# An encoder layer on one core: out-projection sums loaded through GpSimd's queue, the convolution paused at the joint of sample and prompt, and three smaller edits

## The chip, the cores and the metric

One core of a Trainium2 chip runs the whole kernel. Its engines are TensorE (PE, matmuls; PEld is its weight loads), VectorE (DVE), ScalarE (ACT), GpSimd (POOL) and SyncE (SP). Each engine works through its own instructions in order and waits on semaphores. SP here only issues DMAs; ACT and POOL issue some too. The metric is the device time of the kernel in microseconds, the median of several runs.

## The reference

One hybrid encoder layer and a final RMS norm, applied to a prompt of 512 tokens and a sample of 1024 tokens with shared weights, all in float32:

```python
h = rms_norm(x, norm_g)
z = h @ w_in
c_val, c_glu, c_gate, q, k, v, a_gate = jnp.split(z, split_points, axis=-1)
...
conv_out = conformer_conv(c_val, c_glu, w_dw, b_dw, ln_g, ln_b, w_pw) * jax.nn.silu(c_gate)
attn_out = banded_sink_attention(q, k, v, sink) * jax.nn.silu(a_gate)
mix = jnp.concatenate([conv_out, attn_out], axis=-1) @ w_out
return x + mix
```

The model width is 2048, `w_in` has 5632 columns, `w_pw` is 1024x1024 and `w_out` 2048x2048. The convolution is depthwise with 31 taps over `c_val * sigmoid(c_glu)`. Attention has 8 heads of 128, 2 key/value heads and a band of 128 tokens. A final RMS norm with its gain `final_norm_g` follows.

## The kernel before

**Numbers.** Every float32 operand is split into a high and a low part (`parts`, L506: ACT writes the high part, DVE subtracts to get the low one), and each product is three matmul passes: high by high, high by low, low by high. A weight pair of both parts is called `hl`, a token pair `t`.

**Units and jobs.** For the sample and its out-projection, a `Unit` computes a 2x2 block product by seven products instead of eight, P1 to P7, each of 12 matmuls of 128x512. It holds three PSUM banks; P6, P7 and P4 add onto P1's bank, so a bank must be read (`tap`) before the next product onto it. The prompt uses a `Job`: one output block, 48 matmuls over 16 input blocks, with the weights split in two halves (`preps`, L397). The run (L640) is: the sample's input projection in four stages of units (stages 0 to 3), the prompt's jobs `pj` for its input projection, the sample's pointwise jobs, the out-projection units `over[0]` and `over[1]` (eight each, one pass over each half of the inner dimension), the prompt's pointwise jobs, and `last_run` (L1776), the prompt's out-projection with its final norm.

**Sums of two passes.** A unit's result must be added to something. In the input projection the second pass adds the first pass's stored partial with an accumulating DMA on POOL's queue (`add_into`, L500); what follows (scale by the token's norm, sigmoid or silu, store) is put on the list `later` and run by `turn_over` (L542) after `landing` turns (4), one turn per product. At the start of each job the list is flushed entirely. In the out-projection, `Onto` (L270) instead loads the addend first: pass 0 loads the residual x (`xT_s`), pass 1 the stored partial (`part_out`). `begin` (L282) allocates a 128x512 tile, alternately from the pools G and U of four buffers each (`E`, L477), and issues the load on SP. `product` calls it `ahead` products before the one that needs it (2; 0 for the first two units of `over[1]`, which run interleaved). `tap` (L301) then adds the bank onto that tile (L304), and the result is stored on SP.

**Order on the queues.** SP carries nearly every load and store, in an order set when the program is built. Among them are the stores of sums of `w_out` blocks (`wsum_P`, made by DVE at L143 and reused by `last_run`), the token sums (`msum_S`, `mix_d`; L878) and the weights (`raw`).

**Work beside the matmuls.** Three lanes (`Lane`) hold the convolution, the attention and preparations. At each tick a lane gets credit in proportion to its `rate` and emits steps while it has any; `pace` sets a rate at the start of a unit or job. The sample's convolution runs as DVE steps at L1032 and L1040 (128x512 each). Its rate is 0.3 in stage 3 and RATES[3] = 1.0 from the prompt's first job on. `until` forces it to its end at the start of job `pj[18]`.

**The joint.** The sample's last unit is called `end`. During its first four products the prompt's 16 token blocks are split (`follow`, L514 and L515). Its first prompt job has `behind` set: the splits of its weights are ordered behind the last ACT and DVE instructions of the turn before (`marks`). At the start of that job the attention of the sample is put on its lane; its query blocks are loaded by `load_query` (L1145) into U tiles and split on ACT at L510.

**The start.** The constant `norm_g` is loaded first on SP, then the weights and tokens of the first unit; 20 small matmuls (`warm`) run on PE meanwhile.

**The end.** In `last_run` the last product P4 closes rows 2 and 3 of four row blocks, one after the other; rows 0 and 1 wait in `pending`. `complete` (L1730) squares the last quarter, finishes the norm factor `s` with one Newton step, and scales and stores the row in two halves of 128x1024 (L1754 to L1759).

Of the kernel before, what the change touches and what calls it, by code (L numbers as in the profile page):

```python
# [7 lines left out]
F32 = mybir.dt.float32  # L8
F32R = mybir.dt.float32r
AF = mybir.ActivationFunctionType  # L10
ALU = mybir.AluOpType
# [259 lines left out]
class Onto(Unit):  # L271
# [10 lines left out]
    def begin(self, n):  # L282
        if n not in self.d:
            self.d[n] = self.e.E()
            self.e.nc.sync.dma_start(self.d[n], self.source(*n))

    def open(self):
        super().open()
# [97 lines left out]
class Job:  # L386
# [10 lines left out]
    def preps(self, e):  # L397
        def one(k):
            st = {}
            i = slice(k, k + 2 * HALF)  # L400

            def load():
                st["raw"] = e.A([2, HALF, P], F32) if self.early and k else e.raw_tile()
                e.nc.sync.dma_start(st["raw"], self.w[:, i, :])
                if self.low and k:

                    low, c = self.low
                    t = st["hl"] = e.hl_tile()
                    if c == 0:
                        e.nc.sync.dma_start(t[:, 1].bitcast(F32).rearrange("p a b c -> p (a b) c"), low[:, i, :])  # L410
                    else:
                        e.nc.sync.dma_start(t[:, 1, 1].bitcast(F32), low[:, k + HALF : k + 2 * HALF, :])

            def make():
                raw = st.pop("raw")
                if "hl" in st:
                    t = st.pop("hl")
                    e.nc.scalar.activation(t[:, 0], raw, AF.Copy)
                    if self.low[1]:
                        e.nc.vector.tensor_tensor(t[:, 1, 0], raw[:, 0], t[:, 0, 0].bitcast(F32), ALU.subtract)  # L420
                    return t
                t = e.hl_tile()
                e.parts(t[:, 0], t[:, 1], raw)
                return t

            return Prep(load, make, behind=self.behind)

        return [one(self.ks[q]) for q in range(0, len(self.ks), 2 * HALF)]


class Encoder:
# [129 lines left out]
    def constants(self):  # L561
# [4 lines left out]
            nc.sync.dma_start(t, a[key])  # L566
            return t

        self.norm_g = load("norm_g", [ND])
        self.ones = self.const.tile([P, P], F32, name="ones")  # L570
        nc.vector.memset(self.ones, 1.0)
        self.ones_r = self.const.tile([P, P], F32R, name="ones_r")
# [984 lines left out]
class LastPost(Post):  # L1557
# [136 lines left out]
    def load_rows(self):  # L1694
# [4 lines left out]
        self.gain = {}  # L1699
        self.sq = [e.small(4) for _ in range(NB)]  # L1700
        self.rest = [e.small(1) for _ in range(NB)]
        self.load_columns(0, e.A)

    def load_columns(self, c, room):
# [23 lines left out]
    def complete(self, b, c, odd):  # L1728
# [4 lines left out]
        self.seen[b] = n + 1  # L1733
        junk = e.G().rearrange("p (i x) -> p i x", x=P)
        nc.scalar.activation(junk, y, AF.Square, accum_out=self.sq[b][:, n : n + 1])
        if n < 3:
            nc.vector.tensor_tensor(y, y, self.gain[c, odd], ALU.mult)
        sq, rest = self.sq[b], self.rest[b]
        if n == 2:
            nc.vector.tensor_tensor(rest, sq[:, 0:1], sq[:, 1:2], ALU.add)  # L1740
            nc.vector.tensor_tensor(rest, rest, sq[:, 2:3], ALU.add)
            nc.vector.tensor_scalar(rest, rest, 1.0 / D, RMS_EPS, ALU.mult, ALU.add)
        if n == 3:
            s, v, t = e.small(1), e.small(1), e.small(1)
            nc.scalar.activation(s, sq[:, n : n + 1], AF.Sqrt, scale=1.0 / D, bias=rest)
            nc.vector.tensor_scalar(v, sq[:, n : n + 1], 1.0 / D, rest, ALU.mult, ALU.add)
            nc.vector.reciprocal(s, s)
            nc.vector.scalar_tensor_tensor(t, s, s, v, ALU.mult, ALU.mult)
            nc.vector.tensor_scalar(t, t, -0.5, 1.5, ALU.mult, ALU.add)
            nc.vector.tensor_tensor(s, s, t, ALU.mult)  # L1750
            half = self.half
            for h in range(2):
                other, last = (self.blocks(self.rows[b], h, o) for o in (1 - odd, odd))
                nc.scalar.activation(other, other, AF.Identity, scale=s)  # L1754
                if h == c:
                    nc.vector.scalar_tensor_tensor(last, last, s, self.gain[c, odd], ALU.mult, ALU.mult)
                else:
                    nc.vector.tensor_scalar(last, last, s, None, ALU.mult)
                nc.sync.dma_start(self.out[b * P : (b + 1) * P, h * half : (h + 1) * half], self.rows[b][h])  # L1759

    ADDS = {
        "P1": ((0, 0),), "P2": ((0, 0),), "P6": ((0, 1),), "P5": ((1, 1),),
# [12 lines left out]
    def last_run(self, at):  # L1775
# [5 lines left out]
        for c in range(2):  # L1781
            bank = [None] * 3
            for name in ENDS[c]:
# [25 lines left out]
                if end:  # L1809
# [48 lines left out]
def encoder(ctx, tc, a):  # L1858
# [27 lines left out]
    def first():  # L1886
# [273 lines left out]
```

## Time and profile before

| | us |
|---|---|
| median of 3 runs | 2083.21 (2081.64 to 2086.21) |
| profiled execution, its own time | 2080.18 |
| span of its instructions | 2078.4 |
| PE busy | 2060.7 |
| DVE busy | 1754.4 |
| ACT busy | 1043.6 |
| POOL busy | 122.6 |
| mean granted TensorE clock | 0.997 |

The profile is of one execution. A row of a timeline gives start, length, engine, source line, operation, the tiles written and read, and in brackets how long the engine was idle before it and what ended that. Rows of `SPq`, `ACTq` and POOL's `DMA_DIRECT2D` are issues of DMAs, not transfers. The length of a matmul reaches past the start of the next one, so differences of starts are used for rates.

### The profile page before, as it was taken

Reading aid. Unit: us, or ns where it says so; the run is one execution under the profiler, and the core shown is the slowest. Engines: PE = TensorE matmul, PEld = TensorE weight load, DVE = VectorE, ACT = ScalarE, POOL = GpSimd, SP = SyncE. Lnnn points to the kernel's source line nnn. Section 1 sums busy time; section 2 is a strip of 40 time slices with the busy share of each in tenths; the row PEclk is TensorE's granted clock in tenths of the full one; section 3 lists DMA queues with packets and bytes.
Section 4 is the critical chain, followed back from the end, with each engine's and each line's share of the span. In section 5 each row is a group of like instructions: output and inputs, shape, how many; then the busy total and the mean of one; then the engine's idle time right before and its main releaser. Section 6 shows DMA issues by size and latency. Waiting matters only on the chain.

```text
span 2078.4 us, 27092 instructions
## 1 busy us (share of the span) xinstructions
PE 2060.7 (99%) x9259; PEld 1699.2 (82%) x9259; DVE 1754.4 (84%) x2873; ACT 1043.6 (50%) x1711; POOL 122.6 (6%) x176
## 2 busy tenths in 40 slices
PE   9999999999999999999999999999999999999998
PEld 8888888888888888788888888888888887888886
DVE  8767899998899999999666877767799977998887
ACT  7485445333464434554455777336454343454454
POOL 0111111111111111100000000000000000000000
PEclk9999999999999999999999999999999999999999
DMA  8888886864577767954455555996789899678897
GB/s 288 312 298 256 199 223 221 285 220 160 188 242 192 175 169 183 280 166 156 153 172 187 177 182 183 315 330 234 247 289 300 278 299 293 220 247 298 289 333 277
DMA packets 245819, 494.55 MB, mean 238 GB/s; under 512 B 23600, under 2 KB 84400, under 8 KB 245680
## 3 DMA queue, kind: packets, MB, share of 16 engines
q1 hardware_dynamic: 225136, 445.62, 63.9%
q0 software_dynamic: 19392, 45.10, 9.4%
q10 hardware_dynamic: 1152, 2.10, 0.3%
q8 instruction: 72, 1.18, 0.2%
q14 instruction: 67, 0.55, 0.1%
HBM read 331.77 MB, written 160.96 MB: 237 GB/s over the span
## 4 chain that ended last, share of the span: by engine, by line
PE 48%; DVE 7%; issue 6%; DMA 4%; ACT 2%; POOL 1%; SPq 0%; ACTq 0%; POOLq 0%; DVEq 0%
PE a L669 13%; PE a L207 7%; PE c L669 6%; PE b L669 6%; PE c L207 3%; PE pv L1196 2%; PE a L1835 2%; PE s L1167 2%; PE s L1835 2%; PE b L207 1%; PE pt L1201 1%; DVE hl L511 1%; DVE f L1003 1%; DVE t L511 1%; DVE f L1040 1%
## 5 line engine op out<-in xcount | busy, mean ns | idle before, releaser
L207 PE MATMUL a<-t,hl 128*128 128x512 f32 x2640 | 633.6, 391 | 4.7 <-DVE u L304 3.2
L207 PEld LDWEIGHTS a<-t,hl 128*128 128x128 f32 x2640 | 494.7, 188 | 110.6 <-DVE u L304 3.6
L510 ACT ACTIVATE hl<-raw 128x1024 fp32r<-128x1024 f32 (+3 forms) x334 | 296.1, 890 | 384.5 <-PE c L207 81.6
L511 DVE TENSOR_TENSOR hl<-raw,hl 128x1024 fp32r<-128x1024 f32 (+3 forms) x334 | 338.8, 1015 | 145.8 <-ACT hl L510 144.4
L669 PE MATMUL a<-t,hl 128*128 128x512 f32 x1344 | 328.0, 394 | 0.0
L207 PE MATMUL c<-t,hl 128*128 128x512 f32 x1320 | 319.2, 389 | 0.0
L207 PEld LDWEIGHTS c<-t,hl 128*128 128x128 f32 x1320 | 247.3, 188 | 51.6 <-DVE u L304 0.4
L669 PEld LDWEIGHTS a<-t,hl 128*128 128x128 f32 x1344 | 248.6, 188 | 49.8
L1040 DVE SCALAR_TENSOR_TENSOR f<-f,c_w_dw,f 128x512 f32<-128x512 f32 x248 | 173.9, 750 | 0.3
L669 PE MATMUL b<-t,hl 128*128 128x512 f32 x672 | 164.6, 395 | 2.2 <-DVE hl L511 2.2
L1003 DVE SCALAR_TENSOR_TENSOR f<-f,c_w_dw,f 128x512 f32<-128x512 f32 x232 | 163.7, 748 | 1.2 <-ACT f L998 1.2
L669 PE MATMUL c<-t,hl 128*128 128x512 f32 x672 | 164.2, 393 | 0.3 <-DVE hl L511 0.3
L207 PE MATMUL b<-t,hl 128*128 128x512 f32 x660 | 160.0, 389 | 0.0
L669 PEld LDWEIGHTS b<-t,hl 128*128 128x128 f32 x672 | 126.1, 190 | 28.0 <-DVE hl L511 2.6
L669 PEld LDWEIGHTS c<-t,hl 128*128 128x128 f32 x672 | 124.7, 188 | 25.5 <-DVE hl L511 0.7
L207 PEld LDWEIGHTS b<-t,hl 128*128 128x128 f32 x660 | 123.7, 188 | 25.6
L1032 DVE SCALAR_TENSOR_TENSOR f<-f,w_both,f 128x512 f32<-128x512 f32 x120 | 90.0, 750 | 2.1
L236 ACT ACTIVATE u<-a 128x512 f32<-128x512 f32 x82 | 48.7, 594 | 66.8 <-PE a L207 64.2
L236 ACT ACTIVATE g<-a 128x512 f32<-128x512 f32 x78 | 46.3, 594 | 69.1 <-PE a L207 64.6
L1181 ACT ACTIVATE p<-p,tiny 128x384 f32<-128x384 f32 (+1 forms) x96 | 54.5, 570 | 39.8 <-DVE tiny L1178 27.3
L510 ACT ACTIVATE a<-pt 128x512 fp32r<-128x512 f32 x64 | 37.9, 593 | 66.3 <-PE pt L1201 66.2
L511 DVE TENSOR_TENSOR a<-pt,a 128x512 fp32r<-128x512 f32 x64 | 44.1, 689 | 27.3 <-ACT a L510 26.6
(350 smaller groups left out, 2687.9 us busy)
## 6 DMA issues: line engine op xcount, KB each, us to landing
raw<-w_in SPq DMA_DIRECT2D x170, 512.0 KB, 5.3
raw<-w_out SPq DMA_DIRECT2D x31, 512.0 KB, 5.0
raw<-w_pw SPq DMA_DIRECT2D x24, 512.0 KB, 4.2
wsum_P<-raw SPq DMA_DIRECT2D x47, 256.0 KB, 3.3
raw<-wsum_P SPq DMA_DIRECT2D x18, 512.0 KB, 5.0
f<-x_s SPq DMA_DIRECT2D x16, 512.0 KB, 8.2
g<-wsum_P SPq DMA_DIRECT2D x28, 256.0 KB, 4.2
a<-sum_S SPq DMA_DIRECT2D x24, 256.0 KB, 6.2
```

What stands on the lines that cost most here:

```text
L207: nc.tensor.matmul(acc, hl[:, l, o, j, :], toks[j][:, r], start=name in FRESH and j == 0 and q == 0, stop=name in LAST and j == HALF - 1 a ...
L236: nc.scalar.activation(t, bank, AF.Copy)
L510: nc.scalar.activation(hi, x, AF.Copy)
L511: nc.vector.tensor_tensor(lo, x, hi.bitcast(F32), ALU.subtract)
L669: nc.tensor.matmul(job.acc[0], hl[:, l, kk // HALF, kk % HALF, :], r, start=i == 0 and p == 0, stop=i == nk - 1 and p == 2,)
L1003: nc.vector.scalar_tensor_tensor(t, h[:, j : j + T], w(j), t, ALU.mult, ALU.add)
L1032: nc.vector.scalar_tensor_tensor(m0, odd[:, j : j + H], both(j), m0, ALU.mult, ALU.add)
L1040: nc.vector.scalar_tensor_tensor(out, d[:, j : j + H], w(2 * j + k), out if j else m0, ALU.mult, ALU.add)
L1167: nc.tensor.matmul(ps[:, 0:n], qs[:, x, h], k[y][:, keys], start=p == 0, stop=p == 2)
L1181: nc.scalar.activation(p[:, 0:n], p[:, 0:n], AF.Exp, bias=nm[:, h : h + 1], accum_out=l[:, h : h + 1])
L1196: nc.tensor.matmul(pv, v[x][:, vs], pt[:, y], start=i == 0 and p == 0, stop=i == last and p == 2)
L1835: nc.tensor.matmul(acc[t], self.toks[name, m][:, x, i, t * P : (t + 1) * P], parts[i][l].rearrange("p a b -> p (a b)"), start=fresh and fi ...
```

## The change

Seven edits in one diff:

1. `Onto.begin` issues its load on POOL's queue instead of SP's, and the first two units of `over[1]` begin their loads one product ahead instead of none.
2. The convolution's rate is 0 from the start of `end`, and RATES[3] is set at the third prompt job instead of the first.
3. The first half of the first prompt job's weights is no longer ordered behind the marks; the second half still is.
4. `landing` of `end` is 8 instead of 4. The result of its P2, the only one that four turns brought to an end within `end`, is now finished in the flush at the first job's start.
5. `norm_g` is loaded on ACT's queue instead of SP's.
6. 17 warm-up matmuls instead of 20.
7. In `last_run`, the norm factor takes one DVE step less on its chain (the factor -0.5 is folded in ahead, in `less`); scaling is a function of its own, `scale`, which splits the finished half of a row between DVE and ACT and stores it as two quarters, then the other half. Its calls for row 1 and later rows are ordered behind the add and the square of the row that just finished.

```diff
@@ Onto.begin
-            self.e.nc.sync.dma_start(self.d[n], self.source(*n))
+            self.e.nc.gpsimd.dma_start(self.d[n], self.source(*n))
@@ Job.preps
-            return Prep(load, make, behind=self.behind)
+            return Prep(load, make, behind=self.behind and k > 0)
@@ Encoder.constants
-        self.norm_g = load("norm_g", [ND])
+        self.norm_g = self.const.tile([P, ND], F32, name="c_norm_g")
+        nc.scalar.dma_start(self.norm_g, a["norm_g"])
@@ LastPost.complete
+            nc.vector.tensor_scalar(self.less[b], rest, -0.5, None, ALU.mult)
         if n == 3:
             s, v, t = e.small(1), e.small(1), e.small(1)
             nc.scalar.activation(s, sq[:, n : n + 1], AF.Sqrt, scale=1.0 / D, bias=rest)
-            nc.vector.tensor_scalar(v, sq[:, n : n + 1], 1.0 / D, rest, ALU.mult, ALU.add)
+            nc.vector.tensor_scalar(v, sq[:, n : n + 1], -0.5 / D, self.less[b], ALU.mult, ALU.add)
             nc.vector.reciprocal(s, s)
             nc.vector.scalar_tensor_tensor(t, s, s, v, ALU.mult, ALU.mult)
-            nc.vector.tensor_scalar(t, t, -0.5, 1.5, ALU.mult, ALU.add)
-            nc.vector.tensor_tensor(s, s, t, ALU.mult)
...
+            nc.vector.scalar_tensor_tensor(s, t, 1.5, s, ALU.add, ALU.mult)
+            return lambda: self.scale(b, c, odd, s)
+
+    def scale(self, b, c, odd, s):
+        nc, half = self.e.nc, self.half
+        out = self.out[b * P : (b + 1) * P]
+        x, at = self.rows[b][1 - c], (1 - c) * half
+        nc.vector.tensor_scalar(x[:, : half // 2], x[:, : half // 2], s, None, ALU.mult)
+        nc.scalar.activation(x[:, half // 2 :], x[:, half // 2 :], AF.Identity, scale=s)
+        for h in range(2):
+            cols = slice(h * (half // 2), (h + 1) * (half // 2))
+            nc.sync.dma_start(out[:, at + cols.start : at + cols.stop], x[:, cols])
+        other, last = (self.blocks(self.rows[b], c, o) for o in (1 - odd, odd))
+        nc.vector.scalar_tensor_tensor(last, last, s, self.gain[c, odd], ALU.mult, ALU.mult)
+        nc.scalar.activation(other, other, AF.Identity, scale=s)
+        nc.sync.dma_start(out[:, c * half : (c + 1) * half], self.rows[b][c])
@@ LastPost.last_run
-                    for args in pending:
-                        e.urgently(self.complete, *args)
+                    scales = [e.urgently(self.complete, *args) for args in pending]
                     pending.clear()
+                    e.urgently(scales.pop(0))
...
                         finished(t)
-                        e.urgently(self.complete, *pending.pop())
+                        added = nc.cur_bb.bb.instructions[-1]
+                        scales.append(e.urgently(self.complete, *pending.pop()))
+                        squared = self.squared
+                        while scales:
+                            with e.tc.issue_after(added), e.tc.issue_after(squared):
+                                e.urgently(scales.pop(0))
@@ encoder
-        e.warm(20, True)
+        e.warm(17, True)
...
-    end.look = NHL - 1
+    end.look, end.landing = NHL - 1, 8
...
-    pace(pj[0], RATES[3])
+    pace(end, 0.0)
+    pace(pj[2], RATES[3])
...
     for u in over[1][:2]:
-        u.ahead = 0
+        u.ahead = 1
```

More of the change, by code (lines that the diff above doesn't have):

```diff
@@ L1701, in load_rows @@
         self.rest = [e.small(1) for _ in range(NB)]
+        self.less = [e.small(1) for _ in range(NB)]
         self.load_columns(0, e.A)
@@ L1735, in complete @@
         nc.scalar.activation(junk, y, AF.Square, accum_out=self.sq[b][:, n : n + 1])
+        self.squared = nc.cur_bb.bb.instructions[-1]
         if n < 3:
@@ L1745, in complete @@
             nc.scalar.activation(s, sq[:, n : n + 1], AF.Sqrt, scale=1.0 / D, bias=rest)
-            nc.vector.tensor_scalar(v, sq[:, n : n + 1], 1.0 / D, rest, ALU.mult, ALU.add)
+            nc.vector.tensor_scalar(v, sq[:, n : n + 1], -0.5 / D, self.less[b], ALU.mult, ALU.add)
             nc.vector.reciprocal(s, s)
             nc.vector.scalar_tensor_tensor(t, s, s, v, ALU.mult, ALU.mult)
-            nc.vector.tensor_scalar(t, t, -0.5, 1.5, ALU.mult, ALU.add)
[L1750 to L1759, printed above, removed]
+            nc.vector.scalar_tensor_tensor(s, t, 1.5, s, ALU.add, ALU.mult)
[13 more added lines that the diff above has]
+        nc.sync.dma_start(out[:, c * half : (c + 1) * half], self.rows[b][c])
     ADDS = {
```

## The prediction

> **What bounds the kernel now.** I read the page first, then the granted clock by stretches, then TensorE's timeline with the releaser of each wait in brackets, and last the other engines' timelines around those waits and at both ends.
>
> ```profile
> span 2078.4 us, 27092 instructions
> PE 2060.7 (99%) x9259; PEld 1699.2 (82%) x9259; DVE 1754.4 (84%) x2873; ACT 1043.6 (50%) x1711; POOL 122.6 (6%) x176
> ```
>
> TensorE (PE) sets the time: it is busy for all but 17.7 us of the span, start and tail included. A change that removes no matmul can only win what PE loses in waits, in slow clock and at the two ends. The clock by stretches (columns: busy time of PE, weight loads, DVE, ACT, POOL; clock; DMA share; GB/s):
>
> ```profile
> 860.50:864.00 3.50, 3.50 (x10) 2.70 (x9) 3.50 (x6) 1.31 (x2) 0.88 (x1) 0.51 1.05 268
> ...
> 1729.60:1734.30 4.70, 4.63 (x13) 3.66 (x14) 4.37 (x9) 0.74 (x2) 0.00 (x0) 0.64 0.74 238
> ```
>
> The granted clock drops to half in these two places, and PE's timeline shows a wait just before each:
>
> ```profile
> 842.95 3.02 PE L207 MATMUL a<-t,hl 128*128 128x512 f32 x12 [1.07 <-ACT g L236]
> ...
> 1716.53 2.88 PE L207 MATMUL b<-t,hl 128*128 128x512 f32 x12
> 1719.25 2.88 PE L207 MATMUL s<-t,hl 128*128 128x512 f32 x12
> ...
> 859.49 12.36 PE L669 MATMUL b<-t,hl 128*128 128x512 f32 x46 [2.19 <-DVE hl L511]
> 871.69 6.29 PE L669 MATMUL a<-t,hl 128*128 128x512 f32 x27
> ...
> 1729.67 4.43 PE L207 MATMUL a<-t,hl 128*128 128x512 f32 x12 [3.23 <-DVE u L304]
> 1733.89 2.44 PE L207 MATMUL s<-t,hl 128*128 128x512 f32 x9
> ```
>
> A product of 12 matmuls takes 1719.25-1716.53 = 2.72 us, 0.227 a matmul. After the wait of 3.23 us the next 12 take 1733.89-1729.67 = 4.22, so 1.50 more is lost: **4.7 us** at this place, in the out-projection. After the 2.19 us wait 46 matmuls take 12.20 where 46 x 0.227 = 10.44 would do: 1.76 more, **3.95** in all, at the prompt's first job. The wait of 1.07 at 842 is not followed by such a stretch.
>
> The Trainium skill (TensorE: Matmul & The Clock Gate, section "Why this matters for your kernels") warns of idle gaps above about 3 us. By it the gap of 2.19 would cost no clock, and my sum would be 1.8 smaller; the row at 860.50 reads 0.51, so the trace decides against that bound here.
>
> **Part 1: sums loaded on POOL's queue (`Onto.begin`), and one step earlier in two units.** What was late at 1726 was a load, and its queue shows why:
>
> ```profile
> 1718.81 1.57 SPq L504 DMA_DIRECT2D wsum_P<-raw  x2
> ...
> 1721.22 0.39 SPq L504 DMA_DIRECT2D wsum_P<-a  x1
> 1721.67 1.75 SPq L878 DMA_DIRECT2D p<-mix_d  x2
> 1723.46 0.43 SPq L285 DMA_DIRECT2D u<-part_out  x1
> ...
> 1725.37 0.69 DVE L511 TENSOR_TENSOR t<-p,t 128x512 fp32r<-128x512 f32 x1
> 1728.92 0.69 DVE L304 TENSOR_TENSOR u<-a,u 128x512 f32<-128x512 f32 x1 [2.85 <-DMA u<-part_out]
> ```
>
> `u<-part_out` stands on SP behind stores of `wsum_P`, each of which waits for a DVE subtraction (L143). The sum it reads was stored a whole pass earlier, so I put the delay down to the queue. POOL has no other work in this stage. All 64 loads (16 units of 4) move, each freeing SP of an issue like the 0.43 above, which wins nothing by itself. On POOL such a load has no row, so I bound it:
>
> ```profile
> L268 POOL DMA_DIRECT2D part_q<-u x16 | 8.6, 540 | 68.4 <-DVE u L257 61.8 <-ACT u L236 6.6
> L501 POOL DMA_DIRECT2D u<-part_q x16 | 15.0, 940 | 63.0 <-DVE u L257 55.2 <-issue 7.8
> ...
> DMA to landing us min/median/max: 3.8/5.5/9.0
> ...
> u<-part_out SPq DMA_DIRECT2D x16, 256.0 KB, 4.4
> ...
> part_out<-u SPq DMA_DIRECT2D x16, 256.0 KB, 3.1
> ```
>
> An issue costs POOL between 0.54 (a plain store, L268) and 0.94 (an accumulating load, L501), 35 to 60 us in all, on an idle engine. The landing lies between SP's median of 4.4 for the same load and the slowest 9.0 of POOL's accumulating ones (third row, of L501); a plain load is nearest to SP's, and I take 5. The lead: a load is begun two products ahead (5.44), the product itself takes 2.72, and its bank is written again a product later (2.72), less the add's 0.69: 10.2 us. Even 9.0 is covered. In the two interleaved units `ahead` goes from 0 to 1, one step of two products, 5.44 more; the price is a G or U buffer held that much longer, on POOL's own queue.
>
> With the load in time, DVE does L304 at 1726.06 instead of 1728.92; PE has stood since 1729.67-3.23 = 1726.44 and goes on near 1726.7. Of 4.7, 0.3 stays: I take **4.4**. Next DVE could be late: without idle time it is 2.86 ahead of before, while PE is 4.7 ahead, so up to 1.9 could come back. Bounds 2.8 to 4.7.
>
> **Part 2: the joint between sample and prompt.** Four edits meet here: the convolution paused, the first weights freed of their place behind marks (`behind and k > 0`), `landing` 8 for the last sample unit, RATES[3] set at the third job.
>
> ```profile
> 838.89 0.63 ACT L510 ACTIVATE hl<-p 128x512 fp32r<-128x512 f32 x1 [1.15 <-DVE p L143]
> ...
> 842.32 0.57 ACT L236 ACTIVATE g<-a 128x512 f32<-128x512 f32 x1
> ...
> 855.74 0.69 DVE L974 TENSOR_TENSOR g<-g,f 128x512 f32<-128x512 f32 x1 [1.00 <-DMA g<-part_gate]
> 858.21 1.22 DVE L511 TENSOR_TENSOR hl<-raw,hl 128x1024 fp32r<-128x1024 f32 x1
> ...
> L1040 DVE SCALAR_TENSOR_TENSOR f<-f,c_w_dw,f 128x512 f32<-128x512 f32 x10 | 7.2, 750 | 0.0
> ...
> L1032 DVE SCALAR_TENSOR_TENSOR f<-f,w_both,f 128x512 f32<-128x512 f32 x2 | 1.5, 744 | 0.0
> ```
>
> The wait of 1.07 is for ACT's L236, queued behind a weight split that waited 1.15 for DVE, which had convolution steps in front. Without them that wait goes: worth about 1.07, at least 0. The wait of 2.19 is for DVE's L511, the low part of the first weights. DVE idled 1.00 before it for an accumulating DMA: L974 was emitted ahead. With `landing` 8 that sum is finished only in the flush at the job's start, behind L511, and the weights may go earlier: 2.19 and the clock's 1.76 go. Upper bound 1.07+3.95 = 5.0.
>
> Something else is late next. PE would enter the second job at 871.69-5.0 = 866.7. Its weights are ready at:
>
> ```profile
> 865.39 0.63 ACT L510 ACTIVATE a<-u 128x512 fp32r<-128x512 f32 x1 [3.58 <-DMA u<-q_d]
> 865.93 0.71 ACT L514 ACTIVATE t<-a,c_norm_g 128x512 fp32r<-128x512 f32 x1
> ...
> 869.21 1.22 DVE L511 TENSOR_TENSOR hl<-raw,hl 128x1024 fp32r<-128x1024 f32 x1
> ```
>
> ACT stands 3.58 us on the query load `u<-q_d`, and behind it are the prompt's last tokens (L514) and the second job's weights, low part ready at 870.4. The third matmul of that job wants them at 867.1: up to 3.3 late, less 0.6 for a convolution step that leaves DVE's row. I expect two shorter waits (tokens, then weights) of 2.2 together and no halved clock: 5.0-2.2 = **2.8**, bounds 0.3 to 5.0.
>
> The paused work is not gone: the ten L1040 and two L1032 above, 7.2+1.5 = 8.7 us of DVE between 838 and 882, run later. Cover:
>
> ```profile
> 1000.00:1053.00 53.00, 53.00 (x252) 44.10 (x251) 23.72 (x50) 25.38 (x47) 0.00 (x0) 1.00 0.46 149
> ```
>
> DVE is idle for 29 us there, and the forced finish comes only at the prompt's nineteenth job. Without the cover those 8.7 us would stand once in front of a job.
>
> **Part 3: the start.**
>
> ```profile
> 0.74 0.39 SPq L566 DMA_DIRECT2D c_norm_g<-norm_g  x1
> 1.19 0.42 SPq L325 DMA_DIRECT2D raw<-w_in  x1
> ...
> 3.21 0.31 ACT L510 ACTIVATE hl<-raw 128x128 fp32r<-128x128 f32 x1 [1.19 <-DMA raw<-w_in]
> ```
>
> With `norm_g` on ACT's queue every SP issue comes 0.45 earlier. ACT pays one issue, about SP's 0.39, inside its 1.19 of idle time. Three warm-up matmuls fewer make room for it. I take **0.4**, bounds 0 (landing set by bandwidth) to 0.45.
>
> **Part 4: the tail.**
>
> ```profile
> 2072.58 0.16 DVE L1750 TENSOR_TENSOR tiny<-tiny,tiny 128x1 f32<-128x1 f32 x1
> 2072.78 0.72 ACT L1754 ACTIVATE a<-a,tiny 128x512 f32<-128x512 f32 x1 [0.86 <-DVE tiny L1750]
> ...
> 2072.78 0.49 DVE L1758 TENSOR_SCALAR a<-a,tiny 128x512 f32<-128x512 f32 x1
> ```
>
> One tiny step of the chain goes: 2072.78-2072.58 = 0.20, less some 0.06 because the one that stays is a longer form. ACT's two passes stay, so the last store leaves 0.14 earlier; the first bytes leave after DVE's 0.49 instead of ACT's 0.72, with the 0.14 some 0.37 earlier. I take **0.25** between the two. Four more stores cost SP issues, which nothing waits for. The added `less` steps, four of about 0.2, come a product or more before the end, under its matmuls; uncovered they cost 0.8.
>
> **Sum.** 4.4+2.8+0.4+0.25 = 7.85. The profiled execution took 2080.18 (span 2078.4), so it would be 2072.3; the median shown, 2083.21, is 3.0 higher, so **2075.4**. Own range, from the bounds: gains 3.2 (2.8+0.3+0+0.1) to 10.5 (4.7+5.0+0.45+0.37), 2072.7 to 2080.0.
>
> **Rivals.**
>
> A, the wait moves to the second job: the query load holds 2.7 us in one piece and the clock halves again, 1.76. Part 2 gains 0.5, the rest 5.05: 2077.7. For it: ACT's 3.58. Against: tokens come first and split the wait.
>
> B, the load is earlier but the add is not: L304 is placed where it was, behind other DVE work of a saturated engine. Part 1 gains nothing: 2083.21-3.45 = 2079.8. Against: DVE really idled 2.85 for it. With A as well (C): 1.15 left, 2082.1.
>
> D, slower: POOL's loads come late. One mechanism: in POOL's in-order queue a load waits for its buffer's store to land (the 3.1 of `part_out<-u`), then takes the slowest 9.0: 12.1, which is 1.9 beyond the lead of 10.2. Once in each of the second pass's eight units: 15.2 lost, 3.45 won elsewhere, 2095.0. It decides from the second late unit on. For it: 9.0 was seen. Against: the sums are begun in every unit two products ahead.
>
> The Trainium skill (SBUF — State Buffer, "SBUF: two separate sides") says a DMA from GpSimd's queue can wait for descriptors while DVE runs certain copies; that would feed D. In this trace POOL's issues last 0.54 to 0.94 beside a busy DVE.
>
> **How the numbers follow.** Forecast 0.48, A 0.22, B 0.10, C 0.07, D 0.13. About 0.2% (4.2 us) is what a measurement of this kernel can tell from no change. Faster means below 2079.0: forecast and A, 0.70. B and C lie within 4.2 of 2083.21: same, 0.17. Slower is D, 0.13, and it alone is left out of the range, which takes in A, B and C and 2 us below the forecast's own for runs as far apart as those of before (2081.64 to 2086.21): 2070.5 to 2082.5.
>
> **What would show it.** Right: no TensorE wait on L304 near 1720, a clock of 1.00 there, POOL issues through the out-projection, no L1040 between the last unit's start and the third job. Wrong: a wait on `hl` L511 or `t` L515 with the halved clock in the second job (A), a DVE wait on `part_out` issued by POOL (D), L304 still late with its load landed (B).

## The result, and the profile after

The changed kernel takes 2078.75 us (median of 13 runs, 2074.16 to 2084.51) against 2082.3 for the kernel before in the same comparison (13 runs, 2080.57 to 2087.39). The ratio is **0.9979, 95% interval 0.9971 to 0.9987**: 4.4 us faster, 2.7 to 6.0. In a second comparison (`e4_after` below) it is 0.9966 (0.9953 to 0.9978).

The profiled execution of the changed kernel is its fastest, 2074.16 with a span of 2072.4, so the two profiles differ by 6.0 us where the medians differ by less. From its page:

```profile
span 2072.4 us, 27195 instructions
PE 2057.6 (99%) x9256; PEld 1696.0 (82%) x9256; DVE 1752.3 (85%) x2873; ACT 1043.9 (50%) x1711; POOL 157.8 (8%) x240
```

TensorE is 3.1 us less busy with three small matmuls fewer (half clock counts as busy), and POOL has 64 instructions more, the loads. The joint, in TensorE's timeline of the changed kernel:

```profile
843.07 3.01 PE L207 MATMUL a<-t,hl 128*128 128x512 f32 x12 [1.07 <-ACT g L236]
...
858.10 10.50 PE L670 MATMUL b<-t,hl 128*128 128x512 f32 x44 [0.53 <-DVE hl L511]
869.41 0.73 PE L670 MATMUL b<-t,hl 128*128 128x512 f32 x2 [0.81 <-DVE t L515]
```

The wait of 1.07 near 842 has not moved. The wait of 2.19 is 0.53 (the 44 matmuls start 0.227 apart), and a wait of 0.81 for the last token's low part is new. The out-projection, same view, and then the clock over both places (columns as before):

```profile
1705.42 5.72 PE L207 MATMUL a<-t,hl 128*128 128x512 f32 x24 [0.24 <-DVE u L304]
...
1723.30 2.58 PE L207 MATMUL s<-t,hl 128*128 128x512 f32 x10 [0.41 <-DVE hl L511]
```

```profile
857.00:864.00 7.00, 6.47 (x28) 5.05 (x29) 3.60 (x5) 3.01 (x5) 0.88 (x1) 1.00 1.10 310
1722.00:1736.00 14.00, 13.59 (x60) 10.81 (x59) 13.12 (x21) 3.80 (x6) 1.65 (x3) 1.00 0.99 318
```

The wait of 3.23 us is gone, waits of 0.24 and 0.41 are what is left between 1700 and 1745, and the clock is 1.00 at both places. POOL's loads, the group of `begin`'s line in the changed kernel (ns min/median/max, first and last start), and their landing:

```profile
L285 POOL DMA_DIRECT2D u<-part_out x16: 546/546/548, 1683.8 to 1834.4; - x16
...
DMA to landing us min/median/max: 2.7/4.9/6.8
```

On SP the first load of `part_out` started at 1723.46 (in the prediction); on POOL it starts 40 us earlier, at 1683.8.

### The profile page after: what moved, and what is told of

Same layout as the page of the kernel before. It is cut to its first block, busy times and chain, and to the rows that moved or that the text cites. A ratio compares the mean times of both kernels' runs of the same rounds, so it can differ in the third digit from the quotient of the medians.

```text
span 2072.4 us, 27195 instructions
## 1 busy us (share of the span) xinstructions
PE 2057.6 (99%) x9256; PEld 1696.0 (82%) x9256; DVE 1752.3 (85%) x2873; ACT 1043.9 (50%) x1711; POOL 157.8 (8%) x240
## 3 DMA queue, kind: packets, MB, share of 16 engines
q0 software_dynamic: 24512, 61.88, 12.1%
## 4 chain that ended last, share of the span: by engine, by line
PE 52%; issue 7%; DVE 4%; DMA 2%; POOL 1%; ACT 1%; POOLq 0%; ACTq 0%; SPq 0%; DVEq 0%
PE a L670 14%; PE c L670 7%; PE b L670 7%; PE a L207 7%; PE c L207 3%; PE s L1168 2%; PE pv L1197 2%; PE s L1851 2%; PE a L1851 2%; PE b L207 1%; PE pt L1202 1%; DVE hl L511 1%; PE pt L1851 1%; PE pv L1851 1%; POOL u L501 1%
## 5 line engine op out<-in xcount | busy, mean ns | idle before, releaser
L236 ACT ACTIVATE u<-a 128x512 f32<-128x512 f32 x82 | 48.7, 594 | 69.7 <-PE a L207 66.9
L236 ACT ACTIVATE g<-a 128x512 f32<-128x512 f32 x78 | 46.4, 595 | 70.0 <-PE a L207 65.1
L418 ACT ACTIVATE hl<-raw 128x1024 fp32r<-128x1024 f32 x43 | 45.4, 1056 | 47.1 <-PE a L670 18.7
```

The lines of the kernel that those rows point to most:

```text
L236: nc.scalar.activation(t, bank, AF.Copy)
```

## The experiments

All kernels are compared with the kernel before by the same two matmuls of the program, counted among the 128x512 ones. The table gives how much longer (+) or shorter a stretch took than in the first profile of the kernel before; 838 to 905 is the joint, 1700 to 1745 the turn from the first to the second pass of the out-projection. The tail is the time from the last matmul's start to the end of the span. Each ratio is against the kernel before in the same comparison; the stretches are read from one profile each.

| kernel | first product at | joint | out-projection | tail | ratio to before, interval |
|---|---|---|---|---|---|
| before | 5.65 | 0 | 0 | 9.02 | |
| e5_before, again | 5.65 | -0.42 | -0.43 | 8.71 | |
| e1_sums | 5.64 | -2.46 | -4.83 | 9.87 | 0.9968 (0.9956 to 0.9981) |
| e10_queue | 5.65 | +0.51 | -3.73 | 8.74 | 0.9980 (0.9971 to 0.9989) |
| e2_joint | 5.64 | -2.66 | -0.95 | 9.15 | 0.9985 (0.9975 to 0.9994) |
| e3_ends | 5.00 | -1.99 | -0.17 | 9.37 | 0.9989 (0.9981 to 0.9998) |
| changed kernel | 5.01 | -2.82 | -3.46 | 9.21 | 0.9979 (0.9971 to 0.9987) |
| e4_after, again | 5.01 | -2.94 | -3.91 | 9.56 | 0.9966 (0.9953 to 0.9978) |
| e9_no_landing | 5.01 | -1.25 | -3.04 | 9.28 | 0.9974 (0.9964 to 0.9984) |
| e14_no_pause | 5.01 | +1.69 | -3.03 | 9.02 | 0.9989 (0.9979 to 0.9998) |
| e6_pause_early | 5.01 | -4.08 | -2.72 | 9.34 | 0.9968 (0.9956 to 0.9981) |
| e7_no_flush | 5.01 | -4.01 | -2.72 | 9.29 | 0.9958 (0.9944 to 0.9971) |
| e13_both | 5.01 | -4.62 | -1.93 | 9.29 | 0.9957 (0.9943 to 0.9971) |

### The kernel before, once more

> The kernel before, unchanged, for a second profile. In the runs of one part alone the stretch from 40 to 838 us was 1.9 to 3.3 us longer than in the first profile of the kernel before, and the joint, which those runs of edit 1 and of edits 5 to 7 do not touch, lost 2.0 to 2.5 us less: the wait near 859 was 1.95 to 1.99 us there and no half clock followed, where it followed the wait of 2.19. Theory: the kernel before itself varies in the same way, so this profile has waits on L236 near 84, 103 or 163 that the first did not have, and a joint that halves the clock only if its wait is 2.1 us or more. Rival: the first profile is what the kernel before always does, and the longer waits came from the edits.

The kernel before varies from execution to execution, as the theory had it. From 40 to 838 us this execution took 3.6 us longer than the first profile; of that 0.44 and 0.46 were lost at small waits on L236 near 84 and 103. Its joint waited 1.68 us and kept the full clock (by the same brackets e1_sums and e3_ends waited 1.78 and 1.82; the expectation counts from the starts of matmuls). In the out-projection TensorE waited longer than in the first profile:

```profile
1734.86 3.02 PE L207 MATMUL a<-t,hl 128*128 128x512 f32 x12 [3.35 <-DVE u L304]
```

and no half clock followed, against the prediction's reading that such a wait brings one. The windows of this execution around the wait, cut every 3.413 us from the place where its clock halved in the tail, show how the wait lies:

```profile
1729.80:1733.21 3.41, 1.71 (x8) 1.09 (x6) 1.76 (x3) 1.08 (x2) 0.00 (x0) 1.00 0.85 247
1733.21:1736.63 3.42, 1.77 (x8) 1.47 (x9) 2.52 (x5) 1.34 (x3) 0.00 (x0) 1.00 0.83 298
```

The same cut in the first profile of the kernel before, where the half stretches started at 860.55 and 1730.95, 870.40 us or 255 times 3.413 apart:

```profile
857.14:860.55 3.41, 1.22 (x6) 0.89 (x6) 3.41 (x5) 2.38 (x4) 0.86 (x1) 1.00 1.06 330
860.55:863.96 3.41, 3.41 (x10) 2.64 (x9) 3.41 (x6) 1.26 (x2) 0.88 (x1) 0.50 1.04 266
1727.54:1730.95 3.41, 1.28 (x6) 1.06 (x7) 2.03 (x4) 1.15 (x2) 0.00 (x0) 1.00 0.70 251
1730.95:1734.36 3.41, 3.41 (x10) 2.64 (x9) 3.08 (x6) 0.80 (x2) 0.00 (x0) 0.50 0.92 295
```

Six matmuls in a window and the next is at half clock; eight in each of two windows and nothing happens, though the wait was longer. The next kernel measures this by itself.

### Forty holds: what halves the clock

```diff
+    def hold(self):
...
+        nc.tensor.matmul(spin, self.ones_r, self.ones_r, start=True, stop=True)
+        with self.tc.high_priority(URGENT):
+            nc.scalar.activation(z, spin[:, :32], AF.Copy)
+            for _ in range(5 + n % 8):
+                nc.scalar.activation(z, z, AF.Copy)
+        nc.tensor.matmul(spin[:, :32], self.ones_r, z, start=True, stop=True)
```

> The kernel before with 40 holds added to prompt jobs 3 to 42: in the middle of each job TensorE waits for a chain of 6 to 13 small ACT copies before the next product, so that idle times of some 1 to 4 us stand at many phases. It measures the halved clock by itself. In ten profiles so far every half-clock stretch began a whole number of 3.413 us after another, and the stretch ahead of each had 2.0 us or more of idle time inside it (2.0, 2.1, 2.3, 2.5, 3.0), while a wait of 3.5 us that lay across two stretches with 1.87 and 1.78 us halved nothing. Theory: time runs in stretches of 3.413 us on a fixed grid, and a stretch with over 2.0 us of TensorE idle time is followed by one at half clock; all half stretches of this run lie on one grid and idle time per stretch separates halving from not at 2.0 +- 0.1 us. Rival (the length of one gap decides): every single gap above 2.2 us is followed by half clock wherever it lies. Rival (about 3 us decides): only gaps above 3 us are.

The 40 holds and the waits of the kernel itself made 26 stretches at half clock, the tail's among them, every one a whole number of 3.413 us from the tail's start. Three windows of this kernel on that grid, each with the next; the first two are followed by half clock, the third is not:

```profile
987.07:990.48 3.41, 1.39 (x7) 0.94 (x5) 3.40 (x8) 1.89 (x6) 0.00 (x0) 1.00 0.67 229
990.48:993.89 3.41, 0.00 (x0) 0.00 (x0) 3.06 (x7) 3.19 (x15) 0.00 (x0) 0.50 0.15 56
1239.65:1243.07 3.42, 1.60 (x9) 1.16 (x8) 0.00 (x0) 2.13 (x9) 0.00 (x0) 1.00 0.85 261
1243.07:1246.48 3.41, 3.41 (x10) 2.63 (x9) 0.00 (x0) 0.00 (x0) 0.00 (x0) 0.50 0.00 0
1522.96:1526.37 3.41, 1.56 (x8) 1.11 (x6) 0.28 (x1) 1.93 (x8) 0.00 (x0) 1.00 1.00 320
1526.37:1529.79 3.42, 2.83 (x13) 2.35 (x14) 0.00 (x0) 0.47 (x3) 0.00 (x0) 1.00 0.98 303
```

By TensorE's idle time in these rows the theory's border of 2.0 +- 0.1 us fails: the second window was idle for 1.82 us (3.42 less 1.60) and halved the next, the third for 1.85 and did not. Counted by the matmuls' width the border is sharp. At half clock a 128x512 matmul starts every 0.427 us, so at full clock its 512 columns are taken as half of that, 0.213. Over the windows of 14 profiles (from 12 us on, the tail left out) that ran at full clock themselves, the 32 that were followed by half clock hold at most 1.25 us of columns, and the 8412 that were not hold at least 1.24: the border is at about 1.25 us, just under six wide matmuls, where fifteen start in a window without waits (3.413 by 0.227). So it is neither the length of a gap (3.35 us halved nothing, 2.19 did) nor 3 us, but how a gap lies on the grid, and two gaps in one window add up. Both single-gap rivals fall. That it is columns that count and not busy time is seen again in `e13_both`.

### Edit 1 alone, and its queue alone

```diff
-            self.e.nc.sync.dma_start(self.d[n], self.source(*n))
+            self.e.nc.gpsimd.dma_start(self.d[n], self.source(*n))
...
-        u.ahead = 0
+        u.ahead = 1
```

> The kernel before with edit 1 alone: the addends of the out-projection are loaded on POOL's queue, and the first two units of the second pass begin theirs one product ahead. Theory (the load's place in SP's queue is the whole cause): no TensorE wait on L304 above 0.5 us between 1700 and 1740, granted clock 1.00 there, 3.2 to 3.5 us gained at that place and nothing elsewhere, so a profiled execution near 2076.9; the joint keeps its waits of 1.07 and 2.19 us and its half clock. Rival (the gain there needs the other edits, which change when the interleaved units start): the wait of about 3 us on L304 or on L511 comes back, and less than 1.5 us is gained. Rival (POOL's loads are sometimes late): a wait on a load of part_out issued by POOL in the second pass, time no better than before.

> The kernel before with POOL's queue for the addends of the out-projection alone; the first two units of the second pass still begin their loads with the product that needs them (ahead 0). In five profiles with both halves of edit 1 no add L304 waits for a DMA by more than 0.1 us; in the four with the loads on SP each has 3 to 7 such waits. Theory (the queue is the cause, ahead adds a margin that is not needed): no add waits more than 0.3 us for part_out near 1730, the joint of the two passes (1700 to 1745) 2.5 to 4.5 us shorter than in the kernel before. Rival (ahead is the cause): L304 still waits 1 us or more for part_out near 1730, gain there below 1.5 us.

The out-projection is 4.83 shorter with both halves and 3.73 with the queue alone. No wait on L304 above 0.39 us is left there and the clock is 1.00, so the queue is the cause, as the theory of both runs says, and `ahead` is not needed: with the queue alone the first load of `part_out` starts at 1691.5, also some 30 us before SP's. The rest of what was expected of `e1_sums` missed: more was gained there than 3.2 to 3.5, the joint waited 1.78 us instead of 2.19 and kept the full clock, and the profiled execution took 2082.33 instead of 2076.9: against the first profile it lost 2.8 us between 40 and 838 and 5.3 between 1200 and 1700. The group of the adds L304 shows what ended DVE's idle time before them (us, times), first in the second profile of the kernel before:

```profile
  DMA u<-part_out: 3.0, 3
  DMA g<-xT_s: 2.7, 2
...
  DMA u<-xT_s: 1.0, 1
```

then in `e4_after`:

```profile
  PE a L207: 6.7, 9
  PE c L207: 5.4, 4
  PE b L207: 2.0, 1
  PE s L207: 1.7, 1
  PE pt L207: 0.3, 1
```

With SP's queue each of four profiles has three to seven adds that wait over 0.1 us for such a load; with POOL's queue none of nine does. The other terms (`PE`) are waits for the sum itself. `e1_sums` also shows what small waits can cost elsewhere: two of 1.12 and 0.76 us near 1396, in the attention, fell mostly into one window and halved the next, 3.3 us lost. Why they came in this execution stays open.

### Edits 2 to 4 alone, and each without one of them

```diff
-            return Prep(load, make, behind=self.behind)
+            return Prep(load, make, behind=self.behind and k > 0)
...
-    end.look = NHL - 1
+    end.look, end.landing = NHL - 1, 8
...
-    pace(pj[0], RATES[3])
+    pace(end, 0.0)
+    pace(pj[2], RATES[3])
```

> The kernel before with edits 2, 3 and 4 alone: convolution paused, first half of the weights freed of the marks, landing 8. Theory: up to 838 us TensorE runs as before; the wait of 1.07 us on L236 near 842 stays, because the convolution steps before it were emitted ahead of the pause; the wait of 2.19 us falls to about 0.5 with full clock, a wait of about 0.8 us on the last token's L515 appears near 868; 3.2 us gained at the joint and a profiled execution near 2077.0, with the wait of 3.23 us and the half clock in the out-projection as before. Rival (part of what was gained at the joint came from the earlier start of the changed kernel): 2.5 us or less at the joint.

The waits came out as in the changed kernel (1.15, 0.47 and 0.81 us), and the out-projection kept a wait on L304 of 2.53 with its half clock, as expected. The joint is 2.66 shorter than in the first profile, where 3.2 was expected; the ratio gives 3.1 us (1.2 to 5.2). But the five joints without these edits (before, e5, e1, e10, e3) lie between +0.51 and -2.46, mean -0.87, since their wait near 859 runs from 1.68 to 2.98 and the clock halves in two of them only. Against that mean the three with edits 2 to 4 (-2.82, -2.94, -2.66) win **1.9**; none of them halves the clock there.

```diff
-    end.look, end.landing = NHL - 1, 8
+    end.look = NHL - 1
```

> The changed kernel with landing 4 in the sample's last unit, as before; convolution pause and freed weights stay. The prediction's reading: landing 8 is what lets the weights' low part (L511) go ahead of the sum L974 that waited 1.00 us; without it a wait of 1.5 us or more on hl L511 near 858 comes back, and the clock halves if it exceeds 2.1. Rival: freeing the weights of the marks, or the pause, is enough; the wait near 858 stays below 0.7, and the wait of 0.8 on L515 near 868 gets shorter because one sum less stands in the flush.

Without `landing` 8 the wait is back, and in front of it DVE's wait for an accumulating DMA, as the prediction read it. The joint is 1.6 us longer than in the changed kernel's two profiles; the ratios do not tell the two apart. TensorE, then DVE, of this kernel:

```profile
861.49 10.06 PE L670 MATMUL b<-t,hl 128*128 128x512 f32 x43 [1.68 <-DVE hl L511]
```

```profile
857.08 0.69 DVE L975 TENSOR_TENSOR g<-g,f 128x512 f32<-128x512 f32 x1 [1.16 <-DMA g<-part_gate]
```

```diff
-    pace(end, 0.0)
-    pace(pj[2], RATES[3])
+    pace(pj[0], RATES[3])
```

> The changed kernel without its second edit: the convolution keeps its rate in the sample's last unit and RATES[3] is set at the first prompt job, as before; landing 8 and the freed weights stay. The prediction gave the pause the wait of 1.07 us near 842, which stayed in every kernel that pauses at the start of the last unit. Theory: the pause takes ten to twelve convolution steps of about 0.68 us out of DVE's row between 838 and 882, two to four of them ahead of the waits near 858 and 868; without it these two waits grow by 0.7 to 1.5 us together and the joint (838 to 905) is that much longer than in the changed kernel's two profiles. Rival (the pause is idle, landing 8 does it all): DVE waits 2.4 and 1.0 us for DMAs in that flush anyway and the steps fill those waits; the joint is within 0.4 us of the changed kernel's.

The pause is what matters most here; without it the joint is 4.6 us longer than in the changed kernel's two profiles, where the theory said 0.7 to 1.5. TensorE's waits in that stretch add up to 5.97 us against 2.41 and 2.47. TensorE, ACT and DVE of this kernel:

```profile
872.74 5.97 PE L670 MATMUL a<-t,hl 128*128 128x512 f32 x25 [1.96 <-DVE hl L511]
...
879.95 0.85 PE L1168 MATMUL s<-t,a 128*128 128x256 f32 x5 [1.12 <-DVE t L511]
```

```profile
867.06 0.63 ACT L510 ACTIVATE a<-u 128x512 fp32r<-128x512 f32 x1 [3.76 <-DMA u<-q_d]
867.60 1.04 ACT L510 ACTIVATE hl<-raw 128x1024 fp32r<-128x1024 f32 x1
```

```profile
868.34 1.41 DVE L1041 SCALAR_TENSOR_TENSOR f<-f,c_w_dw,f 128x512 f32<-128x512 f32 x2
869.66 0.69 DVE L975 TENSOR_TENSOR g<-g,f 128x512 f32<-128x512 f32 x1
870.26 1.29 DVE L975 TENSOR_TENSOR u<-u,f 128x512 f32<-128x512 f32 x2
871.47 1.22 DVE L511 TENSOR_TENSOR hl<-raw,hl 128x1024 fp32r<-128x1024 f32 x1
```

This is the wait of the prediction's rival A, without its half clock: ACT stands on the query load, and the second job's weights come late in one piece, 1.96 us; the attention behind them waits 1.12 and 0.44 more. The query load is only a part of it: ACT has split the weights at 868.64, and DVE makes their low part only from 871.47, behind two convolution steps (1.41) and three of the delayed sums.

No kernel leaves out edit 3 alone, so what the freed weights are worth by themselves is not known.

### What is left at the joint

```diff
-    pace(end, 0.0)
+    pace(stages[3][-2], 0.0)
```

> The changed kernel with the convolution paused one unit earlier, from the start of the sample's last unit but one. Theory: the wait of 1.07 us on L236 near 842 survived because the convolution steps at 831 to 838 were emitted before the pause; without them DVE's subtractions L143 and ACT's splits L510 behind them come 1.5 us or more earlier and the wait falls below 0.3 us, 0.8 to 1.2 us faster at that place than the changed kernel. Rival: L236 there waits for the splits of the tokens (L514) queued ahead of it on ACT, which wait for nothing of the convolution; the wait stays at 0.9 or more.

The wait near 842 is gone (no bracket at 843.12), and 0.50 appears two products on:

```profile
843.12 3.00 PE L207 MATMUL a<-t,hl 128*128 128x512 f32 x12
...
849.34 3.02 PE L207 MATMUL a<-t,hl 128*128 128x512 f32 x12 [0.50 <-ACT u L236]
```

The joint is 1.2 shorter than in the changed kernel's two profiles (-4.08 against -2.88), as expected; the convolution steps emitted before the pause were the cause of the wait of 1.07.

```diff
-            while self.later:
-                self.turn_over(True)
             job = item[0]
+            while self.later and not job.behind:
+                self.turn_over(True)
```

> The changed kernel with the list of unfinished sums no longer flushed at the start of the prompt's first job; it is flushed at the second. Theory: with landing 8 the sums of part_gate are finished in that flush, ACT and DVE then stand 2.4 and 1.0 us for their accumulating DMAs at 858 to 863, and the last tokens (L514, L515) and the second job's weights stand behind them; without the flush the wait of 0.81 us on L515 near 868 goes and none above 0.4 takes its place, 0.6 to 0.9 us faster at the joint than the changed kernel. The prediction's reading: the tokens are late for the query load (u<-q_d) split on ACT ahead of them; then the wait stays near 0.8.

The changed kernel's ACT timeline shows what the flush does there; L983 is the silu behind the sums:

```profile
861.80 0.63 ACT L983 ACTIVATE u<-u 128x512 f32<-128x512 f32 x1 [2.48 <-DVE u L975]
863.47 0.64 ACT L983 ACTIVATE u<-u 128x512 f32<-128x512 f32 x1 [1.03 <-DVE u L975]
...
864.90 1.06 ACT L418 ACTIVATE hl<-raw 128x1024 fp32r<-128x1024 f32 x1 [0.80 <-ACT u L983]
865.87 0.61 ACT L510 ACTIVATE a<-u 128x512 fp32r<-128x512 f32 x1
```

The query's split at 865.87 waited for nothing; ACT's time went to the sums. Without the flush the second job runs through (no bracket at 872.01):

```profile
861.45 10.72 PE L670 MATMUL b<-t,hl 128*128 128x512 f32 x46 [0.49 <-DVE hl L511]
872.01 6.29 PE L670 MATMUL a<-t,hl 128*128 128x512 f32 x27
```

ACT still stands 2.66 us on the query load in this kernel, and TensorE waits for nothing behind it. The joint is 1.1 shorter, but 905 to 1200 is 1.2 longer than in the changed kernel's two profiles, in waits of the attention near 914 to 917.

Both edits together:

> The changed kernel with the convolution paused one unit earlier and without the flush at the prompt's first job. Each alone made the joint (838 to 905) about 1.2 us shorter than the changed kernel's two profiles; the second gave 1.2 back between 905 and 1200. Theory: the waits of 1.07 us near 842 and 0.81 near 868 are independent and both go, the joint is 2.0 to 2.5 us shorter than in the changed kernel, median 1 to 2.5 us below its ratio of 0.9966. Rival: what the one frees runs into what the other moved (ACT and DVE are behind there anyway), joint no more than 1.4 us shorter.

The joint is 1.7 shorter than in the changed kernel's two profiles, between theory and rival. The ratio, 0.9957, is not apart from 0.9958 without the flush alone. Both are clear of the kernel before; that they beat the changed kernel is not shown, since the intervals overlap. The profile of this kernel took 2.8 us more than the first one between 1900 and 1960, where the clock halved after a window in which TensorE was 3.08 us busy:

```profile
1913.14:1916.55 3.41, 3.08 (x22) 2.64 (x21) 1.87 (x4) 1.56 (x2) 0.00 (x0) 1.00 0.92 282
1916.55:1919.97 3.42, 3.42 (x10) 2.65 (x9) 3.04 (x8) 2.05 (x4) 0.00 (x0) 0.50 1.08 379
```

```profile
1913.55 1.84 PE L701 MATMUL s<-ones,f 128*128 128x1 f32 x16
1915.25 0.48 PE L1851 MATMUL a<-hl,t 128*128 128x512 f32 x1
1916.06 1.25 PE L1851 MATMUL a<-hl,t 128*128 128x512 f32 x3 [0.33 <-DVE f L1594]
```

Sixteen column sums of one column each fill 1.7 us and hold almost no columns; with a wait of a third of a microsecond beside them the window holds 0.97 us of columns, and the next is at half clock. The second profile of the changed kernel has the same sums at 1911 without the wait, 1.52 us of columns in their window, and keeps its clock.

### The ends alone, and the changed kernel again

Edits 5, 6 and 7 of the change, nothing else; and then the changed kernel unchanged.

> The kernel before with edits 5, 6 and 7 alone: norm_g on ACT's queue, 17 warm-up matmuls, the new tail. Theory: the first matmul of the first product comes 0.6 us earlier and TensorE leads by about 1.1 us at 40 us, but small new waits in the sample's input projection (near 347, 608, 808 and 828) give it back before 857, because TensorE there runs into DVE and ACT; the tail is 0.2 us longer from the last matmul to the end; together within 0.4 us of the kernel before. Rival (the lead of the start holds to the end and the waits seen in the changed kernel came from its other edits): 0.9 us faster than before. Prediction's own numbers: 0.4 at the start and 0.25 at the tail, 0.65 faster.

The first product comes at 5.00 instead of 5.65. The ratio says 2.3 us faster (0.4 to 4.0): the prediction's 0.65 and the rival's 0.9 both lie in it, so the time settles neither. The claim that the waits near 608, 808 and 828 give the lead back falls: they stand in `e5_before`, which has no lead. On the mean the eight profiles with these edits are 0.6 us ahead of the five without at 40 us, and from there to 838 they lose no more than the others (2.55 and 2.65 us against the first profile). The tail is no shorter (9.37).

> The changed kernel itself, once more. Its profiled execution was the fastest of its 13, 4.6 us below their median, and several of the others show a mean granted clock of 0.998 instead of 0.999, which is what one stretch of 3.41 us at half clock makes of 2078 us. Theory: in some executions a wait of the joint or of the out-projection grows to the size that halves the clock; a profile of such an execution shows one half-clock stretch inside the span and a wait of over 1.5 us ahead of it. Rival (the spread is spread over the kernel, many waits of DMAs a little longer): time of 2077 to 2081 with no half-clock stretch except at the tail.

This execution has no half clock inside its span and took 2077.62, as the rival had it: it lost 2.7 us between 40 and 838 against 1.2 in the first profile of the changed kernel. Other executions do read 0.998, but so does the profile of `e6_pause_early`, where only the tail is at half clock, so that reading does not tell whether a stretch inside the span was halved. Over the runs of that comparison the mean clock is 0.9986 for the changed kernel (5 runs) and 0.9970 for the one before (22 runs): 0.0016 of 2087, an estimate of **3.3 of the 7.1 us**, is clock. One window of 3.413 us at half clock is 0.0008 of such a mean, so the kernel before has about two more of them in a mean execution.

By their times alone the parts cannot be told from the whole. In that comparison edit 1 alone has 0.9968 and the changed kernel 0.9966, and the gains of `e1_sums`, `e2_joint` and `e3_ends`, 6.7, 3.1 and 2.3, add up to 12.1 where the whole has 7.1; the intervals allow that. What edits 2 to 7 add is read from the stretches, not from a time.

## Why the prediction was right, and where it was wrong

The time, 2078.75, lies in the range 2070.5 to 2082.5 and in the forecast's own, 2072.7 to 2080.0; the direction is right. The gain of 7.85 was too large: 4.4 here, 7.1 (4.6 to 9.8) in the second comparison. The four parts as the profiles give them below, 2.9, 1.9, 0.6 and -0.2, add up to 5.2.

**Out-projection, 4.4.** The mechanism is right and so is the queue as the cause. Nine profiles with the loads on POOL have a mean of -3.26 at that place, four with them on SP -0.39: 2.9, near the low bound of 2.8. The mis-sized term is the wait that stays: 0.3 was taken, and the nine have 0.93 us of waits between 1700 and 1745 on the mean (0 to 1.85), on adds of DVE and on weight splits of DVE and ACT, where the four with SP have 3.13. This is the lateness of DVE that the bounds allowed for and the sum left out. The 1.50 of half clock was counted as if it always came: it stands in three of the four profiles with SP, in none of the nine with POOL, and `e5_before` waited 3.35 us there without it. An issue costs POOL 0.546, a load lands after 4.9 where 5 was taken, the slowest after 6.8.

**Joint, 2.8.** -2.82 in the profile is close by luck: the wait of 1.07 stayed, and less came late behind it than was taken. Against the mean of the joints without these edits it is 1.9. The half clock of 1.76 is again a draw and not a fixed price: two of those five joints have it, none of the eight with any of the edits. Three steps of this part:

- "Without them that wait goes: worth about 1.07" failed. The pause begins with `end`, and the steps ahead of 842 were emitted before (`e6_pause_early`). What the pause is worth lies behind it: 4.6 us, at the second job and the attention behind it, where the prediction took 0.6 "for a convolution step that leaves DVE's row".
- `landing` 8 takes the sum out of the weights' way: held (`e9_no_landing`).
- "Something else is late next", 2.2 in two shorter waits behind the query load: it was one of 0.81, beside the 0.53 left of the old one, behind the sums of the flush instead (`e7_no_flush`). The query load makes TensorE wait only without the pause (`e14_no_pause`).

**Start, 0.4.** The first product comes 0.64 earlier, above the bound of 0.45, which counted SP's place alone; 0.64 is three warm-up matmuls of 0.213, which ended just ahead of that product in both kernels. By the rows of ACT its tokens were split at 5.39 before and at 4.64 in the changed kernel, so the earlier loads were needed for it too; neither edit was tried alone.

**Tail, 0.25.** Failed. Five tails without edit 7 have a mean of 9.10, eight with it 9.30. The chain did get shorter; SP's last issues, in the kernel before and in the changed one:

```profile
2074.14 0.33 SPq L1759 DMA_DIRECT2D y_p<-f  x1
```

```profile
2067.48 0.39 SPq L1769 DMA_DIRECT2D y_p<-f  x1
```

From the last matmul's start (2069.40 and 2063.18) that is 4.74 and 4.30 us. Both stores land 3.31 later, but from that landing to the end of the program it is 0.96 us in the kernel before and 1.60 in the changed one. The five profiles without edit 7 have 0.96 to 0.98 there, the eight with it 1.22 to 1.67; SP passes six waits from the last landing to its drain, where two stood before. So the step that failed is "Four more stores cost SP issues, which nothing waits for", as far as the rows show; that the extra stores put the waits there was not tried.

**Rivals.** A doesn't happen with the pause; without it its wait comes, but no half clock. B falls, and C with it: L304 came with its load. D falls: POOL itself waits for the stores that free its buffers (7.88 and 6.75 us before its loads at 1702.98 and 1710.28 in the changed kernel), but no add waited for a POOL load in nine profiles.

## What to carry to other kernels

Before a load's lateness is put down to its transfer, read what stands ahead of its issue on its queue; here an idle engine's queue removed every such wait for 0.55 us of issue each. Side work is paused where its steps are emitted, not where the wait shows: look which unit emitted the steps that stand in front. A price read in one execution, above all a halved clock, is one draw; a second profile of the kernel before shows which terms of the sum are chances.

## What the hardware showed that I had not expected

In the 14 profiles the clock is decided on a grid of 3.413 us: a window with under about 1.25 us of matmul columns is followed by one at half clock, up to 1.7 us lost. The grid lies differently in each execution, so a wait of 2.19 us cost that and one of 3.35 nothing, two waits of about a microsecond added up within a window, and sixteen matmuls of one column counted for next to nothing. The Trainium skill (TensorE: Matmul & The Clock Gate, section "What's actually happening") has a free-running window of 3413 ns, and the trace agrees with it; by its table the slow state comes after an idle window, and here a window with columns for over a third of its time (1.25 of 3.413 us) is enough.
